# A two-layer decoder trunk with 32 experts: fewer slot groups, an earlier place for the norms' vectors, early fetches of the next layer's weights

## The chip, the cores and the metric

The kernel runs on one core of one Trainium2 chip. The metric is the device time of the whole program in microseconds (us), here the median of several runs.

## The reference, cut to what matters

Two layers work on 256 tokens of 1024 channels. In each, a token-mixing sublayer (one wide projection, two attentions, two gates, two branch projections and an output projection) is followed by a layer norm; then comes the channel sublayer, on which this change works:

```python
g_val, g_idx = lax.top_k(g_prob, 1)                 # one of 4 groups
e_val, e_idx = lax.top_k(e_prob, 2)                 # two of its 8 experts
for g in range(4):
    hg = silu(x @ w_g[g]) * (x @ w_u[g])            # 8 experts, 1024 -> 256
    y = y + (hg * comb[:, g]) @ w_d[g]              # 256 -> 1024
ple = sigmoid(x @ w_ple_gate) * (p @ w_ple)
x = layer_norm(alpha * x + y + ple, ln2_g, ln2_b)
```

So each layer has 32 experts, and each of the 256 tokens goes to two of them. All 32 experts' weights are read in each layer, 3 MB each.

## The kernel before, in words

**Places.** Nearly all of the on-chip memory is an arena of 47 places (`Arena`, L59; `Held`, L132), each as large as one weight tile of 512 KB. A tile that is to be loaded (`load=True`) takes the place that was given back longest ago, in the order of the program; any other takes one of the youngest free places, the fifth from the end. A transfer into a place can start only when the last reader of the former tenant is done. All weight transfers are issued on one queue, SP's, in the order of the program, so a transfer that waits for its place holds up all behind it.

**Slots and groups.** Tokens are gathered into 128 slots at a time, one group of experts. An expert has 64 or 32 slots, so a group is a pair (2 x 64) or a quad (4 x 32). The first `NFIX` experts (6) are taken by number, so that their weights can be fetched before the routing is known. The other experts are ranked by their number of tokens; those up to `NBIG` (12) get 64 slots, the others 32 (L878 to L889). That makes six pairs and five quads, eleven groups. `order` sets their order: P0 P1 P2 Q P3 Q P4 Q P5 Q Q. If an expert has more tokens than slots, `leftover` (L1183) runs loops over all experts; with these inputs it has nothing to do. Counted with the reference's own routing, the experts after the first four, ordered by tokens, have 45, 39, 28, 25, then at most 23 in the first layer and 39, 39, 33, 32, then at most 28 in the second; the first six have at most 45.

**A pass.** The loop at L1204 makes one pass for each group `gi`. In a pass TensorE (PE) does the gate and up products of the next group (`front(gi+1)`, L1126, which frees 4 tiles of each expert as it goes), the down products of this group (`back(gi)`, L1141, 2 tiles of each expert), the gather of the group after the next (`gather`, L899, into a place of its own), and the sum into the output (`combine`, L1068). A pair has 12 tiles, a quad 24, and PE's work on either is the same. The loads of ranked experts (`fetch`, L1030) are issued as `front` and `back` come to them in the program. In some passes (`early`, `e1`, `lastat`) units of the per-layer embedding are done as well (`Embed`, L732): two or three tiles for each quarter of the channels, a unit for each quarter and each half of the tokens. `e1` is pass 2; before, `early` is passes 4, 5, 6. In pass `ifat` (3) every engine branches on whether `leftover` has work.

**Around it.** Before the passes the fixed experts' tiles are fetched (L1111), then `nemb` further embeddings (L1116). In the pass before the last, `wide` (L379) takes two places for the last norm's gain and bias, loads 4 KB for each into one partition, and GpSimd (POOL) spreads them. `back(last)` (L1145) fetches the last group's down tiles. In the first layer it then fetches the first four tiles of the next layer's projection (`ahead`, L1147); after the norm's first steps ACT and POOL split these into the two parts that PE multiplies (L1271). `wide` also serves the first norm (L712), beside the router's weights `wr36` (L713).

Of the kernel before, what the change touches and what calls it, by code (L numbers as in the profile page):

```python
# [21 lines left out]
D = 1024  # L22
S = 256
DEPTH = 2
P = 128
KT = D // P
# [15 lines left out]
FAR = 1000.0  # L42


NFIX = 6
NBIG = 12


SEC = ["iq", "sq", "sk", "sv", "dq", "dk", "dv", "ga0", "ga1", "gb0", "gb1"]
# [30 lines left out]

@with_exitstack
def tile_hybrid_trunk(ctx: ExitStack, tc: tile.TileContext, x_in, xT_in, pT_in, pos_in, ws, wik, wrt, lnv,
                      brt, lamv, sublnv, out, places=47, t2b=4, young=4, gsb=1, hTb=1, silb=2, nring=5, early=(4, 5, 6), nahead=4, apart=8, npre=36, wA=1, wB=1, wC=1, wD=1, wE=3, inorder=2, e0=2, e1=2,  nearly_=0, peng_=1, ifat=3, im=0, df=0, dh=15, nol=0, diag=1, rpool='0000', lastemb=1, lastat=6, pre_if=(4,5), npair=6, fh=False, fg=0, order=(0,1,2,6,3,7,4,8,5,9,10), engs=None, nemb=1, nwarm=9, nfine=2, nah=4, o1=False, o2=False, o3=True, o4=True, order2=True, pa=2, pb=7, f1=True):
    nc = tc.nc
    V, A, G = nc.vector, nc.scalar, nc.gpsimd

    class Tensor:

        last = None
# [17 lines left out]
    def in_turn():  # L107

        return tc.issue_after(PE.last.ins)
# [14 lines left out]
    def bank():  # L124
        return ps.tile([P, 512], F32, tag="mm", bufs=4, name=nm("mm"))
# [6 lines left out]
    class Held:  # L132
# [11 lines left out]
        def free(self):  # L144
            arena.give(self.b)
# [16 lines left out]
    def load(l, i, shape):  # L162
        r = Held(shape, load=True)
        nc.sync.dma_start(r.t, ws[l, i])
        return r
# [41 lines left out]
    def split(hi, lo, src, eng=V):  # L207
        copied[0] = A.activation(hi, src, AF.Copy)  # L208
        copied[1] = eng.tensor_tensor(lo, src, hi, op=OP.subtract)  # L209
# [12 lines left out]
    ahead, ready = [], []  # L222
    nearly, peng = nearly_, peng_
# [30 lines left out]
    def constants():  # L254
# [14 lines left out]
        G.iota(kbon, pattern=[[-1, NE]], base=NE - 1, channel_multiplier=0, allow_small_or_imprecise_dtypes=True)  # L269
        V.tensor_scalar(kbon[:, :NFIX], kbon[:, :NFIX], 1.0e6, None, op0=OP.add)  # L270
        G.iota(kid[:, 0:1], pattern=[[0, 1]], base=0, channel_multiplier=1, allow_small_or_imprecise_dtypes=True)
        V.tensor_scalar(kid[:, 1:2], kid[:, 0:1], float(NFIX), 1.0e6, op0=OP.is_lt, op1=OP.mult)
        V.tensor_tensor(kid[:, 1:2], kid[:, 1:2], kid[:, 0:1], op=OP.subtract)
# [52 lines left out]
    def parts(w, ring=None, eng=V, old=False):  # L326

        if ring:
            ring.append(ring.pop(0))
        r = Held([2, 512], F32R, load=old, place=ring[-1] if ring else None)  # L330
        split(r.v[:, 0, :], r.v[:, 1, :], w, eng)
        return r
# [45 lines left out]

    def wide(i, l):  # L379

        r = Held([D])
        nc.sync.dma_start(r.v[0:1], lnv[l, i:i + 1])
        G.partition_broadcast(r.v, r.v[0:1])  # L383
        return r
# [68 lines left out]
    for l in range(DEPTH):  # L453
# [3 lines left out]
        ahead, ready = [], []  # L457
# [240 lines left out]
        for h in range(2):  # L698
# [10 lines left out]
            if h == 0:  # L709
                free(*gates[:2])  # L710
        free(yaT, ybT)
        lng, lnb = wide(0, l), wide(1, l)  # L712
        wr36 = Held([KT, 36])  # L713
        nc.sync.dma_start(wr36.v, wrt[l])
        o = [None, None]
        for h in range(2):
# [151 lines left out]
        def places_of(b, mask, cols):  # L868

            n = cols.stop - cols.start  # L870
            PE.matmul(b[:, 0:n], trib, mask[:, 0, :], start=True, stop=True)
            PE.matmul(b[:, n:2 * n], onesb, mask[:, 0, :], start=True, stop=False)
            PE.matmul(b[:, n:2 * n], trib, mask[:, 1, :], start=False, stop=True)
            V.scalar_tensor_tensor(posm[:, :, cols], mask, -FAR, b[:, :2 * n].rearrange("p (t e) -> p t e", t=TT),
                                   op0=OP.mult, op1=OP.add)


        groups = [[(r, 2, 64)] for r in range(0, 2 * npair, 2)]  # L878
        small = NBIG
        for r in range(2 * npair, NBIG):  # L880
            n = min(2, NE - small)
# [42 lines left out]
        def marks_of(gi):  # L924

            gs = wt([P, TT, P], F32, "gs", gsb)
            c = 0
            for r, n, w in groups[gi]:
                marked[0] = V.tensor_tensor(gs[:, :, c:c + n * w].rearrange("p t (e s) -> p t e s", e=n),
                                            iom[:, None, None, :w].to_broadcast([P, TT, n, w]),  # L930
                                            posm[:, :, r:r + n, None].to_broadcast([P, TT, n, w]), op=OP.is_equal)
                c += n * w
            return gs
# [17 lines left out]
        places = bank()  # L951
# [5 lines left out]
        with in_turn():  # L957
            places_of(places, mkf[:, :, :NFIX], slice(0, NFIX))
        gs = marks_of(0)
        with tc.issue_after(marked[0].ins):  # L960
# [24 lines left out]
            V.tensor_scalar(perm, iom[:NE, :NE], FAR, kcol[:, 2:3], op0=OP.add, op1=OP.is_equal)  # L985
            V.tensor_copy(cw[:, :, :NFIX], cbf[:, :, :NFIX])
        with in_turn():
# [8 lines left out]
        cmi = ids[:, NE:]  # L996
        V.tensor_scalar(ids[:, :NFIX], iom[0:1, :NFIX], FAR, None, op0=OP.add)
        V.tensor_copy(ids[:, NFIX:NE], b[0:1, 2 * NE + NFIX:3 * NE])
        over = cut(NE, rows=1)
        for c, n in (slice(0, NBIG), 64.0), (slice(NBIG, NE), 32.0):  # L1000
            V.tensor_scalar(over[:, c], b[0:1, 3 * NE + c.start:3 * NE + c.stop], n, None, op0=OP.subtract)
# [40 lines left out]
        def weights_of(gi, js):  # L1042
            for j in js:
                for r, _ in experts(gi):
                    if (r, j) not in fetched:
                        fetch(r, j)
            return [[fetched.pop((r, j)) for r, _ in experts(gi)] for j in js]
# [15 lines left out]
        def halves_of(yp):  # L1063
            y = t2([P, 512], F32R), t2([P, 512], F32R)
            split(*y, yp)
            return y
# [48 lines left out]
                        fetch(r, j)  # L1115
        for q in range(1, 1 + nemb):  # L1116
            emb[q] = Embed(q)

        def strips(gi):


            for i, (_, sl) in enumerate(experts(gi)):
                for c in range(sl.start, sl.stop, 32):
                    yield i, slice(c, c + 32)
# [16 lines left out]
        def back(gi, hT):  # L1141

            ysplit.clear()
            ysplits.clear()
            wr = weights_of(gi, range(4, 6))  # L1145
            if gi == last and l < DEPTH - 1:
                ahead.extend(load(l + 1, i, [2, 512]) for i in range(len(ahead), KT // 2))  # L1147
                ready.extend(parts(r.v[:, k, :], eng=G) for r in ahead[:nearly] for k in range(2))
            ys = []
            for h in range(2):  # L1150
                yp = bank()
                for f in range(2):
                    for i, sl in strips(gi):
                        PE.matmul(yp[sl, :], hT[:, f, sl], wr[f][i].v[:, h, :], start=f == 0, stop=f == 1)
                ys.append(halves_of(yp))
                ysplits.append(copied[0])
                ysplit.append(copied[1])
            free(*wr[0], *wr[1])
            return ys

        last = len(groups) - 1
# [21 lines left out]
        def leftover(most):  # L1183
            def onward(cols, n):
                V.tensor_scalar(posm[:, :, cols], posm[:, :, cols], float(n), None, op0=OP.add)

            with tc.If(most > 0, preferred_fallthrough_block=False):
                onward(slice(0, NBIG), -64)
                onward(slice(NBIG, NE), -32)
                with tc.For_i(0, 2, 1):  # L1190
                    with tc.For_i(0, NE, 1) as r:
                        rest(r)
                    onward(slice(0, NE), -P)
                onward(slice(0, NBIG), 64 + 2 * P)
                onward(slice(NBIG, NE), 32 + 2 * P)
# [8 lines left out]
        for gi in range(len(groups)):  # L1204
# [31 lines left out]
            if gi == last - 1:  # L1236
                lng, lnb = wide(2, l), wide(3, l)
                xn = [Held([D]) for _ in range(TT)]
                if l < DEPTH - 1:
                    xT = Split(KT)  # L1240
# [102 lines left out]
```

## Time and profile before

| | |
|---|---|
| time, median of 3 runs | 939.35 us (938.26 to 940.98) |
| the profiled execution, its own time | 940.85 us |
| its span, first to last instruction | 939.2 us |
| PE busy | 906.3 us (96%) |
| VectorE (DVE), ScalarE (ACT), POOL busy | 425.7, 347.9, 33.8 us |
| read from HBM | 278.70 MB, 298 GB/s over the span |
| mean granted TensorE clock | 0.994 |

How to read it: busy time of PE counts a matmul from its start to a modelled end, so a PE that works through small pieces as they arrive still looks busy. The mean rate of the transfers covers stages of very different load: the attention needs few weights, the experts need most of them. In the timelines a row is a run of like instructions: its start, its length, engine, line, operation, output and inputs, count, and in brackets the idle time before it with what ended that.

### The profile page before, as it was taken

The page shows a single profiled execution, that of the slowest core. Times are in us where ns is not written, and L with a number is a line of the kernel's source. Part 1 is how long each engine was busy: PE and PEld are TensorE (multiplying, and loading weights), DVE is VectorE, ACT ScalarE, POOL GpSimd, SP SyncE. Part 2 cuts the span into 40 slices and gives each one's busy share as a digit, 9 for nine tenths or more (in the row PEclk, how much of TensorE's full clock was granted, in tenths as well). Part 3 has the DMA queues.
Part 4 walks back from the last instruction along what each step waited for, and adds up shares of the span by engine and source line. Part 5 has one row for each costly group of instructions (what it writes and reads, how often), then busy time and mean ns, then how long its engine had stood idle before and what let it go on. Part 6 is the DMA issues. An engine that isn't in the chain of part 4 may idle for free. (4 is left out here: it accounts for less than half of the span.)

```text
span 939.2 us, 15942 instructions
## 1 busy us (share of the span) xinstructions
PE 906.3 (96%) x5761; PEld 604.4 (64%) x5761; DVE 425.7 (45%) x1068; ACT 347.9 (37%) x704; POOL 33.8 (4%) x37
## 2 busy tenths in 40 slices
PE   8999999999999999999899999999989999999994
PEld 5877777876556466554388777788855465666441
DVE  6797466775221111122468954668731212112124
ACT  6567676532211111111346666775221111111110
POOL 0000000000000000000410000001000000000010
PEclk9999999999999999999999999999999999999998
DMA  8995343777899999996999233357778999999943
GB/s 280 414 405 202 115 144 127 248 235 286 304 380 385 412 418 416 416 415 273 387 418 364 90 125 123 113 186 252 251 278 322 360 417 414 418 419 416 418 177 139
DMA packets 79013, 280.86 MB, mean 299 GB/s; under 512 B 9160, under 2 KB 9928, under 8 KB 78928
## 3 DMA queue, kind: packets, MB, share of 16 engines
q1 hardware_dynamic: 78784, 279.78, 77.9%
q8 instruction: 47, 0.77, 0.3%
q14 instruction: 38, 0.31, 0.1%
q10 hardware_dynamic: 144, 0.00, 0.0%
HBM read 278.70 MB, written 1.05 MB: 298 GB/s over the span
## 5 line engine op out<-in xcount | busy, mean ns | idle before, releaser
L92 PE MATMUL acc<-a,a 128*128 128x512 f32 x1440 | 352.3, 398 | 2.7 <-ACT a L208 2.0
L92 PEld LDWEIGHTS acc<-a,a 128*128 128x128 f32 x1440 | 265.7, 188 | 65.5 <-ACT a L208 3.3
L92 PE MATMUL mm<-a,a 128*32 128x512 f32 (+5 forms) x1776 | 237.6, 526 | 0.0
L208 ACT ACTIVATE a<-a 128x512 fp32r<-128x512 f32 (+1 forms) x247 | 150.7, 631 | 100.2 <-PE acc L92 69.2
L209 DVE TENSOR_TENSOR a<-a,a 128x512 fp32r<-128x512 f32 (+1 forms) x239 | 160.1, 690 | 51.2 <-ACT a L208 50.5
L92 PEld LDWEIGHTS mm<-a,a 128*32 128x32 f32 (+3 forms) x1776 | 110.7, 130 | 99.2 <-issue 86.8
L92 PE MATMUL mm<-a,hT 128*32 128x512 f32 x704 | 96.4, 603 | 8.8 <-DMA a<-ws 4.9
L92 PEld LDWEIGHTS mm<-gs,a 128*128 128x128 f32 x704 | 80.4, 192 | 17.2 <-PE mm L92 11.7
L92 PE MATMUL mm<-gs,a 128*128 128x128 f32 x704 | 84.7, 278 | 0.0
L1050 ACT ACTIVATE sil<-mm 128x256 f32<-128x256 f32 x22 | 8.4, 383 | 171.5 <-PE mm L92 156.2
L92 PEld LDWEIGHTS mm<-a,hT 128*32 128x32 f32 x704 | 25.3, 111 | 71.4 <-issue 55.9
L1051 DVE SCALAR_TENSOR_TENSOR sil<-sil,wsl,mm 128x256 f32<-128x256 f32 x22 | 10.6, 481 | 133.6 <-ACT sil L1050 133.4
L209 DVE TENSOR_TENSOR t<-mm,t 128x512 fp32r<-128x512 f32 x44 | 30.4, 692 | 68.6 <-ACT t L208 68.6
L208 ACT ACTIVATE t<-mm 128x512 fp32r<-128x512 f32 x44 | 26.3, 597 | 78.6 <-PE mm L92 78.6
L919 DVE CAST sT<-mm 128x256 fp32r<-128x256 f32 x22 | 9.3, 425 | 97.4 <-PE mm L92 97.4
L92 PE MATMUL acc<-t,sT 128*128 128x512 f32 x176 | 48.4, 410 | 0.0
L906 ACT ACTIVATE a<-mm 128x512 f32<-128x512 f32 x40 | 23.9, 597 | 50.1 <-PE mm L92 47.6
L92 PEld LDWEIGHTS acc<-t,sT 128*128 128x128 f32 x176 | 31.1, 189 | 9.0 <-issue 2.5
L763 DVE TENSOR_TENSOR sil<-sil,mm 128x256 f32<-128x256 f32 x16 | 6.7, 416 | 54.4 <-ACT sil L762 54.4
L548 ACT ACTIVATE t<-mm,mx 128x128 f32<-128x128 f32 (+1 forms) x64 | 26.0, 421 | 10.7 <-DVE mx L545 10.7
L762 ACT ACTIVATE sil<-mm 128x256 f32<-128x256 f32 x16 | 6.1, 383 | 63.7 <-PE mm L92 63.7
L383 POOL PARTITION_BROADCAST a<-a x8 | 10.6, 1356 | 511.0 <-DMA a<-lnv 279.6
(197 smaller groups left out, 644.6 us busy)
## 6 DMA issues: line engine op xcount, KB each, us to landing
a<-ws SPq DMA_DIRECT2D x523, 512.0 KB, 9.4
a<-x_in SPq DMA_DIRECT2D x2, 512.0 KB
out<-a SPq DMA_DIRECT2D x4, 256.0 KB, 2.7
a<-xT_in SPq DMA_DIRECT2D x3, 256.0 KB
a<-wik SPq DMA_DIRECT2D x2, 288.0 KB, 8.2
a<-ws SPq DMA_DIRECT2D x2, 256.0 KB, 4.3
pT<-pT_in SPq DMA_DIRECT2D x2, 256.0 KB
a<-wrt SPq DMA_DIRECT2D x2, 144.0 KB, 2.7
```

The costliest lines, as they stand in the source:

```text
L92: self.last = nc.tensor.matmul(*a, **k)
L208: copied[0] = A.activation(hi, src, AF.Copy)
L209: copied[1] = eng.tensor_tensor(lo, src, hi, op=OP.subtract)
L383: G.partition_broadcast(r.v, r.v[0:1])
L548: A.activation(e[:, i * nk:(i + 1) * nk], b[:, i * nk:(i + 1) * nk], AF.Exp, bias=mx[:, i:i + 1], accum_out=sums[i])
L762: A.activation(g, b[:, :256], AF.Sigmoid)
L763: V.tensor_tensor(g, g, b[:, 256:], op=OP.mult)
L906: A.activation(xg, b.rearrange("p (k s) -> p k s", k=4), AF.Copy)
L919: V.tensor_copy(sT, b[:, :2 * P].rearrange("p (t q) -> p t q", t=TT))
L1050: A.activation(sil, gu[:, :FE], AF.Sigmoid)
L1051: V.scalar_tensor_tensor(sil, sil, wsl, gu[:, :FE], op0=OP.mult, op1=OP.mult)
```

## The change

It alters the sizes and the order of the groups (four fixed experts, eight with 64 slots: four pairs and six quads, in the order P0 P1 P2 Q P3 Q Q Q Q Q), moves the embedding units one pass forward, fetches three further embeddings instead of one before the first pass, fetches the next layer's first four tiles there too, and lets `wide` and `wr36` take the longest free place.

```diff
-NFIX = 6
-NBIG = 12
+NFIX = 4
+NBIG = 8
...
-def tile_hybrid_trunk(..., early=(4, 5, 6), lastat=6, npair=6, order=(0,1,2,6,3,7,4,8,5,9,10), nemb=1, ...):
+def tile_hybrid_trunk(..., early=(3, 4, 5), lastat=5, npair=4, order=(0,1,2,4,3,5,6,7,8,9), nemb=3, ...):
...
     def wide(i, l):
-        r = Held([D])
+        r = Held([D], load=True)
         nc.sync.dma_start(r.v[0:1], lnv[l, i:i + 1])
         G.partition_broadcast(r.v, r.v[0:1])
...
-        wr36 = Held([KT, 36])
+        wr36 = Held([KT, 36], load=True)
...
         for q in range(1, 1 + nemb):
             emb[q] = Embed(q)
+        if l < DEPTH - 1:
+            ahead.extend(load(l + 1, i, [2, 512]) for i in range(KT // 2))
...
             wr = weights_of(gi, range(4, 6))
-            if gi == last and l < DEPTH - 1:
-                ahead.extend(load(l + 1, i, [2, 512]) for i in range(len(ahead), KT // 2))
-                ready.extend(parts(r.v[:, k, :], eng=G) for r in ahead[:nearly] for k in range(2))
             ys = []
```

(`nearly` is 0, so the last of the removed lines did nothing.)

## Rows read from the trace of the kernel before

**Rows 1.** The page: PE's busy time; the weight tiles' issues, median us to landing.
```profile
PE 906.3 (96%) x5761; PEld 604.4 (64%) x5761; DVE 425.7 (45%) x1068; ACT 347.9 (37%) x704; POOL 33.8 (4%) x37
...
a<-ws SPq DMA_DIRECT2D x523, 512.0 KB, 9.4
```
**Rows 2.** Timeline of PE: where fronts begin, and one back (408.23).
```profile
401.34 7.07 PE L92 MATMUL mm<-a,a 128*32 128x512 f32 x64
408.23 3.62 PE L92 MATMUL mm<-a,hT 128*32 128x512 f32 x32
...
418.19 2.35 PE L92 MATMUL mm<-a,a 128*32 128x512 f32 x20
...
765.81 1.90 PE L92 MATMUL mm<-a,a 128*32 128x512 f32 x10
...
811.95 1.90 PE L92 MATMUL mm<-a,a 128*32 128x512 f32 x10
...
839.17 1.90 PE L92 MATMUL mm<-a,a 128*32 128x512 f32 x10
```
**Rows 3.** Timeline of PE: the last group's down products and what follows, both layers.
```profile
459.37 0.73 PE L92 MATMUL acc<-t,sT 128*128 128x512 f32 x2
...
466.39 0.66 PE L95 MATMUL mm<-identr,a 128*128 128x128 f32 x4 [1.28 <-DVE a L414]
...
913.47 1.05 PE L92 MATMUL mm<-a,hT 128*32 128x512 f32 x2
...
918.01 1.04 PE L92 MATMUL mm<-a,hT 128*32 128x512 f32 x2 [1.61 <-DMA a<-ws]
...
922.97 2.76 PE L92 MATMUL mm<-a,hT 128*32 128x512 f32 x18 [0.16 <-DMA a<-ws]
925.66 2.22 PE L92 MATMUL acc<-t,sT 128*128 128x512 f32 x8
```
**Rows 4.** Timeline of SP's queue: start, length, line, tile and count of the issues.
```profile
217.08 0.33 SPq L164 DMA_DIRECT2D a<-ws  x1
228.87 91.40 SPq L1040 DMA_DIRECT2D a<-ws  x68
...
444.74 0.58 SPq L382 DMA_DIRECT2D a<-lnv  x2
445.54 3.11 SPq L1040 DMA_DIRECT2D a<-ws  x6
448.69 2.38 SPq L164 DMA_DIRECT2D a<-ws  x4
...
691.48 90.79 SPq L1040 DMA_DIRECT2D a<-ws  x68
...
815.05 78.07 SPq L1040 DMA_DIRECT2D a<-ws  x62
911.21 0.59 SPq L382 DMA_DIRECT2D a<-lnv  x2
912.02 3.12 SPq L1040 DMA_DIRECT2D a<-ws  x6
```
**Rows 5.** Stretches: length, busy time of each engine, PE clock, DMA share, GB/s.
```profile
228.90:288.90 60.00, 58.26 (x513) 30.32 (x505) 12.38 (x35) 10.91 (x20) 0.00 (x0) 1.00 0.89 327
288.90:436.90 148.00, 145.91 (x1084) 88.40 (x1084) 28.22 (x75) 25.96 (x54) 0.00 (x0) 0.99 1.03 415
...
691.50:751.50 60.00, 58.26 (x513) 30.32 (x505) 12.37 (x35) 10.91 (x20) 0.00 (x0) 1.00 0.88 328
751.50:899.50 148.00, 146.13 (x1075) 90.03 (x1072) 27.89 (x71) 26.43 (x56) 0.00 (x0) 1.00 1.02 416
```
**Rows 6.** Short stretches, with the same columns, and a PE row behind a wait.
```profile
312.00:316.00 4.00, 2.27 (x12) 0.69 (x16) 1.32 (x3) 0.17 (x1) 0.00 (x0) 0.72 1.03 410
...
916.00:920.00 4.00, 2.16 (x6) 0.27 (x4) 0.00 (x0) 0.00 (x0) 0.00 (x0) 1.00 0.96 339
...
313.73 5.31 PE L92 MATMUL mm<-a,hT 128*32 128x512 f32 x32 [2.09 <-DVEq L1187]
```

More of the change, by code (lines that the diff above doesn't have):

```diff
@@ L82, in tile_hybrid_trunk @@
 def tile_hybrid_trunk(ctx: ExitStack, tc: tile.TileContext, x_in, xT_in, pT_in, pos_in, ws, wik, wrt, lnv,
-                      brt, lamv, sublnv, out, places=47, t2b=4, young=4, gsb=1, hTb=1, silb=2, nring=5, early=(4, 5, 6), nahead=4, apart=8, npre=36, wA=1, wB=1, wC=1, wD=1, wE=3, inorder=2, e0=2, e1=2,  nearly_=0, peng_=1, ifat=3, im=0, df=0, dh=15, nol=0, diag=1, rpool='0000', lastemb=1, lastat=6, pre_if=(4,5), npair=6, fh=False, fg=0, order=(0,1,2,6,3,7,4,8,5,9,10), engs=None, nemb=1, nwarm=9, nfine=2, nah=4, o1=False, o2=False, o3=True, o4=True, order2=True, pa=2, pb=7, f1=True):
+                      brt, lamv, sublnv, out, places=47, t2b=4, young=4, gsb=1, hTb=1, silb=2, nring=5, early=(3, 4, 5), nahead=4, apart=8, npre=36, wA=1, wB=1, wC=1, wD=1, wE=3, inorder=2, e0=2, e1=2,  nearly_=0, peng_=1, ifat=3, im=0, df=0, dh=15, nol=0, diag=1, rpool='0000', lastemb=1, lastat=5, pre_if=(4,5), npair=4, fh=False, fg=0, order=(0,1,2,4,3,5,6,7,8,9), engs=None, nemb=3, nwarm=9, nfine=2, nah=4, o1=False, o2=False, o3=True, o4=True, order2=True, pa=2, pb=7, f1=True):
     nc = tc.nc
```

## The prediction, made before the changed kernel was run

> **What bounds the kernel now.** I read the page first: PE is busy for 96% of the span [rows 1], so the first guess is that PE's work is the time. Then I went through PE's timeline pass by pass. A pass without embedding takes 16.85 us (418.19 less 401.34), one with two embedding units 27.2 (839.17 less 811.95) [rows 2], and between them PE hardly waits. There are two exceptions. In the branch of pass 3 PE stands for 2.09 us [rows 6]. And the last `back`, which begins at 913.47 in the second layer and needs 3.62 us of matmuls [rows 2, 3], is not done before 925.66, because it waits for its tiles one at a time [rows 3]. SP's queue tells why: the 62 issues that start at 815.05 are over at 893.1, nothing is issued until 911.21, then come the two loads of the norm's vectors, and only then the last six weight tiles [rows 4]. `wide` had taken young places, which the second last `back` was still reading. The queue stood still for 18 us while places were free. The first layer does the same at 444.74.
>
> The queue itself comes next. In each layer the ranked loads begin when the ranks are known, which I call T0: 228.87 and 691.48 [rows 4]. In the 148 us that follow the first 60 it moved 415 and 416 GB/s [rows 5], which is 117 tiles of 0.524 MB, a pitch of 1.262 us a tile. In the first 60 us it moved 327 and 328 GB/s, 37.4 tiles, which would have taken 47.2 us at the pitch: 12.8 us were lost to the start and to places not yet free [rows 5]. So from T0 + 60 on the queue is full, and PE's lead over it is small. That is the state the change meets.
>
> **The change part by part.**
> *One group fewer.* It takes a pass of 16.85 us from PE in each layer. The experts and their bytes stay.
>
> *Four fixed experts instead of six.* Twelve tiles move behind T0: the queue now has 28 x 6 = 168 to bring there, 212.0 us at the pitch. Before it had 156 and five of embeddings. These five (`nemb`) and, in the first layer, the four of the next layer move ahead of T0, where the queue is idle anyway from 217.4 to 228.87 [rows 4]; twelve fixed tiles leave it, so T0 stays. They hold places, though. At the first pass the tenants were 36 fixed tiles, 5 of embeddings and 4 of activations: 2 of 47 free. Now they are 24 + 10 + 4, and 4 more in the first layer: 5 free there, 9 in the second.
>
> *What is lost at the start.* With 3 places more at T0 the queue gets three tiles further before it waits for PE, 3.8 us: 9.0 us lost in the first layer. With 7 more it is 8.8: 4.0 lost in the second. A second wait is new. Front(4) begins 74.3 us behind T0 (765.81 [rows 2]); pass 3 now holds the branch and two embedding units, 29.3 us, so front(5) begins at T0 + 103.6 and frees its first tiles 1.8 us later. The places given until then allow 5 + 48 (fronts) + 20 (backs) + 5 (embeddings) - 1 (the gathered slots) = 77 loads in the first layer and 81 in the second, and at its pitch the queue lands the 77th at 9.0 + 97.2 = 106. It runs nearly dry: two to four us. I take four, since the step from landing to matmul isn't in the sum otherwise. Bounds for all of this: 4.0 us in either layer without any further wait, or 12.8 + 4 in both.
>
> *The norms' vectors.* Their loads now find a free place and cost SP two short issues. What they held up by 18 us follows at once. What is late next is the queue's own pitch.
>
> *The last `back`.* After its last tile 2.7 us of matmuls remain (925.66 less 922.97 [rows 3]). So it ends at 228.87 + 212.0 + 9.0 + 4 + 2.7 = 456.6 in the first layer, where it was 459.37 [rows 3], and at 691.48 + 212.0 + 4.0 + 4 + 2.7 = 914.2 in the second, where it was 925.66. That is 2.8 and 11.5, together 14.3 us. PE alone would be through earlier by 22 and 13 us: 913.47 with 3.62 of matmuls and about 1 of the sum in between is 918 without the wait, 7.7 earlier than now; less 16.85 that is 901.2, and 434.8 in the first layer. So the queue bounds the last passes: a quad brings 24 tiles, 30.3 us, to 16.85 us of PE.
>
> *Next layer's first tiles.* Their fetch leaves the place at 448.69 [rows 4]. Behind the last `back` PE waits for DVE's norm (1.28 us at 466.39 [rows 3]), not for these tiles, so I cost their earlier arrival at nothing; without that cover it would be worth about a microsecond. *The first norm's vectors and router weights* lie before T0, where PE has no wait for a transfer: nothing. *Two more value loads a layer, other masks and limits, units a pass earlier*: nothing, SP needs about 0.5 us for an issue (3.11 for six [rows 4]) of the 1.262, and the units are as many as before. `leftover` stays empty, by the token counts.
>
> **The sum**: 940.85 us for the profiled execution less 14.3 is 926.5; the median of the runs lies 1.5 lower, so 925.0.
>
> A rule speaks against all this. The Trainium skill, "DMA: Bandwidth & Descriptors", section "Where 436 GB/s comes from", says that transfers from HBM are bound at about 358 GB/s for each core. By that 168 tiles would take 246 us, an estimate, the kernel would be at about 993, and no pass should have been taken off PE. The rows of the same queue with the same tiles show 415 and 416 [rows 5]; the measurement decides, and I give it no chance.
>
> **The rivals.**
> *Places run out* (0.10). The embeddings and the next layer's tiles hold 11 places that experts could use, and the extra free places help nothing: 12.8 + 4 us lost in both layers. Then the ends are 460.4 and 923.0, in all 1.7 us better: 937.6. For it: the queue does lose 12.8 us today [rows 5]. Against it: the first wait is counted in places, and there are more of them.
>
> *PE's clock* (0.07), the slower one. In the last passes PE starves, and the granted clock falls to the lower of its two levels, 1.2 of 2.4 GHz. A pass then takes up to 33.7 us, more than the 30.3 of its tiles, so PE is the bound again: 3.4 us in each of up to five starved passes, and 2.7 more behind each last tile, 22 in all, 947. It decides where the waits of a pass come in one piece, as in the branch of pass 3, and not one for each tile. For it: behind the 2.09 us wait the clock was 0.72 and 32 matmuls took 5.31 instead of 3.62 us [rows 2, 6]. Against it: from 916 to 920 PE was busy for 2.16 of 4 us at a clock of 1.00 [rows 6], since it had a piece to do for each tile that came. The Trainium skill, "TensorE: Matmul & The Clock Gate", Part 1 on the HAM clock gate, says that throttled is the default and activity releases it, which the 0.72 bears out and the 1.00 at half activity does not decide.
>
> *PE stays the bound* (0.02). The queue keeps up, and the kernel gains the 16.85 us and the 7.7 of the wait in each layer: 890. It would need 1.15 us a tile; no stretch shows it.
>
> *The change doesn't do what it says* (0.01): an expert overflows its slots and `leftover` runs, far slower. The counts exclude it for these inputs.
>
> **The numbers.** The forecast has 0.80. A measurement of this kernel can tell about 0.3%, 2.8 us, from no change. Faster: forecast and PE-bound, 0.82. Same: places run out, 0.10. Slower: clock and overflow, 0.08. The range: with 4.0 us lost in each layer and no second wait the gain would be 27.3, 912; I stop at 914. Above it takes in the rival of the places: 938.
>
> **What would show it.** PE's timeline should have ten fronts a layer; SP's queue no gap before the vectors, and 168 weight issues from T0 almost without one, at 415 GB/s until the end; the last passes should show PE waiting for tiles; the last `back` should end near 456 in the first layer and, counted from T0, 223 us behind it in the second. Wrong would be: gaps in the queue behind T0 + 60, a clock below 1 in the last passes, or a T0 that moved.

## The result, and the profile after

The changed kernel takes 929.11 us (median of 4 runs, 927.96 to 930.78) against 940.16 us for the kernel before on the same chip (4 runs): a ratio of 0.9883, with a 95% interval from 0.9856 to 0.9911. That is 11 us faster, where 14.3 were forecast. The profiled execution took 929.02 us and its span is 927.1 us, 12.1 shorter than before.

SP's queue first, in the timeline of the changed kernel: start, length, line, tile and count of the issues. These rows answer to [rows 4].

```profile
229.16 205.53 SPq L1040 DMA_DIRECT2D a<-ws  x160
435.57 1.53 SPq L382 DMA_DIRECT2D a<-lnv  x2
438.45 7.52 SPq L1040 DMA_DIRECT2D a<-ws  x8
446.07 0.37 SPq L466 DMA_DIRECT2D a<-wik  x1
...
689.57 201.51 SPq L1040 DMA_DIRECT2D a<-ws  x160
891.98 1.51 SPq L382 DMA_DIRECT2D a<-lnv  x2
894.52 7.78 SPq L1040 DMA_DIRECT2D a<-ws  x8
```

The queue no longer stands still for the vectors: 891.08 to 891.98 is all that lies between the weights and them. The 168 loads are there, T0 is where it was in the first layer (229.16, 228.87 before), and the next layer's first load is issued right behind the last expert's.

What the queue moved, by stretches of the changed kernel from T0 (length, busy times, PE clock, DMA share, GB/s in the last column), and one stretch of the last passes:

```profile
229.20:289.20 60.00, 58.26 (x513) 30.33 (x505) 12.38 (x35) 10.92 (x20) 0.00 (x0) 1.00 0.95 355
289.20:445.90 156.70, 150.96 (x1014) 83.10 (x1011) 26.07 (x71) 23.72 (x50) 2.48 (x2) 1.00 1.02 411
689.60:749.60 60.00, 58.26 (x513) 30.32 (x505) 12.39 (x35) 10.92 (x20) 0.00 (x0) 1.00 0.99 393
749.60:902.20 152.60, 148.60 (x1036) 86.39 (x1033) 26.68 (x72) 24.57 (x52) 2.38 (x2) 1.00 1.01 405
...
424.00:456.00 32.00, 28.74 (x132) 6.48 (x125) 2.56 (x6) 2.42 (x6) 2.48 (x2) 1.00 1.03 417
```

The first 60 us behind T0 now bring 355 and 393 GB/s, where they brought 327 and 328 [rows 5]. In tiles that is 40.6 and 45.0 of the 47.5 that the pitch of 1.262 us allows: 8.7 and 3.2 us are lost. In the last passes the queue runs at 417 GB/s without a hole, and PE does only 132 matmuls in 32 us; a pass without embedding does 144 in 16.85 us.

PE's timeline of the changed kernel in these passes (in brackets the idle time before a row and what ended it):

```profile
406.92 1.89 PE L92 MATMUL mm<-a,hT 128*32 128x512 f32 x6
409.03 1.04 PE L92 MATMUL mm<-a,hT 128*32 128x512 f32 x2 [0.22 <-DMA a<-ws]
410.29 1.04 PE L92 MATMUL mm<-a,hT 128*32 128x512 f32 x2 [0.22 <-DMA a<-ws]
...
454.35 2.76 PE L92 MATMUL mm<-a,hT 128*32 128x512 f32 x18 [0.18 <-DMA a<-ws]
457.05 0.73 PE L92 MATMUL acc<-t,sT 128*128 128x512 f32 x2
...
910.87 2.76 PE L92 MATMUL mm<-a,hT 128*32 128x512 f32 x18 [0.17 <-DMA a<-ws]
913.56 2.22 PE L92 MATMUL acc<-t,sT 128*128 128x512 f32 x8
```

From about 407 on in the first layer PE catches up with the queue in every pass. Then it uses each tile the moment it lands (two matmuls of 1.04 us, 0.2 us of waiting, one piece in 1.26 us, the queue's pitch) until the pass has other work for it, as from 416.8 to 427.9. The page of the changed kernel counts such a PE as busy, so its share is 96% as before [rows 1], though another resource sets the time:

```profile
PE 890.8 (96%) x5473; PEld 588.1 (63%) x5473; DVE 421.2 (45%) x1056; ACT 341.9 (37%) x692; POOL 33.4 (4%) x37
```

The 288 matmuls fewer than before [rows 1] are one pass of 144 in each layer, so the kernel does ten passes, and `leftover` has run none of its loops. The last `back` ends at 457.05 (459.37 before [rows 3]) and, in the second layer, 224.0 us behind T0 (234.2 before).

### The profile page after: what moved, and what is told of

The parts are those of the page before. It is cut to its first block, busy times and chain, and to the rows that moved or that the text cites. A ratio compares the mean times of both kernels' runs of the same rounds, so it can differ in the third digit from the quotient of the medians.

```text
span 927.1 us, 15397 instructions
## 1 busy us (share of the span) xinstructions
PE 890.8 (96%) x5473; PEld 588.1 (63%) x5473; DVE 421.2 (45%) x1056; ACT 341.9 (37%) x692; POOL 33.4 (4%) x37
## 5 line engine op out<-in xcount | busy, mean ns | idle before, releaser
L92 PE MATMUL mm<-a,a 128*32 128x512 f32 (+5 forms) x1648 | 229.2, 521 | 1.1 <-DMA a<-ws 1.1
L92 PEld LDWEIGHTS mm<-a,a 128*32 128x32 f32 (+3 forms) x1648 | 107.4, 132 | 96.9 <-issue 78.2
L92 PE MATMUL mm<-a,hT 128*32 128x512 f32 x640 | 102.5, 594 | 10.1 <-DMA a<-ws 5.2
L92 PEld LDWEIGHTS mm<-gs,a 128*128 128x128 f32 x640 | 73.1, 192 | 15.5 <-PE mm L92 10.9
L92 PE MATMUL mm<-gs,a 128*128 128x128 f32 x640 | 77.0, 278 | 0.0
L209 DVE TENSOR_TENSOR t<-mm,t 128x512 fp32r<-128x512 f32 x40 | 27.7, 692 | 78.3 <-ACT t L208 78.3
L208 ACT ACTIVATE t<-mm 128x512 fp32r<-128x512 f32 x40 | 23.9, 597 | 87.8 <-PE mm L92 87.8
L92 PE MATMUL acc<-t,sT 128*128 128x512 f32 x160 | 43.9, 410 | 0.0
L906 ACT ACTIVATE a<-mm 128x512 f32<-128x512 f32 x36 | 21.5, 597 | 45.2 <-PE mm L92 43.9
L92 PEld LDWEIGHTS acc<-t,sT 128*128 128x128 f32 x160 | 28.3, 189 | 7.4 <-DVE t L209 0.9
```

What stands on the lines that cost most here:

```text
L92: self.last = nc.tensor.matmul(*a, **k)
L906: A.activation(xg, b.rearrange("p (k s) -> p k s", k=4), AF.Copy)
```

## The experiments

Times of different experiments come from different runs, so they are compared by their ratio to the kernel before, and finer differences by the traces, counted from each layer's own T0. The stage ahead of the first T0, which most edits leave alone, put T0 between 229 and 232 in these traces; what moves it was not looked into.

**The vectors alone.** The kernel before, with eleven groups and six fixed experts, and only this edit:

```diff
-        r = Held([D])
+        r = Held([D], load=True)
...
-        wr36 = Held([KT, 36])
+        wr36 = Held([KT, 36], load=True)
```

> The kernel before, with nothing changed but the places of the norms' vectors and the router weights. Theory (the changed kernel gains because the queue no longer stands still, and is then bound by the queue, so that the pass taken from PE is worth little): the last back ends where PE's own work ends it, 7.7 us earlier in each layer (about 451.6 and 918.0 less 7.7), 924.8 in all against 940.2, so faster than the changed kernel's 929.1. Rival (the pass of 16.85 us taken from PE makes the gain): at most 3 us faster than before, 937 or more.

Measured: 926.31 us, a ratio of 0.9841 (0.9823 to 0.9859). In PE's timeline of this kernel, at the end of either layer:

```profile
448.56 3.64 PE L92 MATMUL mm<-a,hT 128*32 128x512 f32 x32
452.13 0.73 PE L92 MATMUL acc<-t,sT 128*128 128x512 f32 x2
...
907.73 3.64 PE L92 MATMUL mm<-a,hT 128*32 128x512 f32 x32
911.30 2.25 PE L92 MATMUL acc<-t,sT 128*128 128x512 f32 x8
```

The last `back` does its 32 matmuls in one piece, 3.64 us, without a wait. It ends 222.7 us behind T0 in the first layer, where before it ended 230.5 behind, and 226.5 in the second, where it was 234.2: 7.8 and 7.7 us. The edit also moves the first norm's vectors and the router weights, but the stretch that holds them, from the first layer's last `back` to the second T0, takes 232.7 us instead of 232.1, and the first T0 is no earlier (229.45, 228.87 before): the gain is not there. These two arguments alone give as much as the whole change or more; the intervals of the two ratios just touch (0.9859 and 0.9856), and by the traces the span is 2.2 us shorter.

**The change without the vectors.** The changed kernel with these two edits undone.

> The changed kernel, with the vectors and the router weights back in young places. Theory: the vectors' loads wait for the second last back, which ends at about 447 in the first layer and 903 in the second, and the six to eight tiles behind them follow then: the last back ends some 4 to 6.5 us later in each layer, 937 to 942. Rival (the pass taken from PE makes the gain): 929 to 932.

Measured: 938.06 us, a ratio of 0.9963 (0.9944 to 0.9982). SP's queue in the first layer of this kernel:

```profile
419.75 20.91 SPq L1040 DMA_DIRECT2D a<-ws  x17
449.44 0.58 SPq L382 DMA_DIRECT2D a<-lnv  x2
450.24 4.18 SPq L1040 DMA_DIRECT2D a<-ws  x6
```

The hole is back, 440.7 to 449.4, and in the second layer 899.7 to 908.9. The last `back` ends 233.8 and 227.9 us behind T0, 5.9 and 3.9 later than in the changed kernel. All the rest of the change, a pass of PE's work in each layer among it, is worth 3.5 us or so without the two edits, and nothing on top of them. So the gain is the vectors', and the rival that gave it to the group is out. What the pass alone would be worth stays open: no run takes it without the twelve tiles that move behind T0 with it.

**The next layer's tiles late.** In the changed kernel:

```diff
-        if l < DEPTH - 1:
-            ahead.extend(load(l + 1, i, [2, 512]) for i in range(KT // 2))
...
             wr = weights_of(gi, range(4, 6))
+            if gi == last and l < DEPTH - 1:
+                ahead.extend(load(l + 1, i, [2, 512]) for i in range(KT // 2))
```

> The changed kernel, with the next layer's first four tiles fetched at the last back again. Theory (places at T0 decide what the queue loses at the start): the first layer has 9 places instead of 5, loses 4 us instead of 9 and ends its last back at about 452 instead of 457; the four tiles land at about 452, ten us before PE uses them, so about 924. Rival (the early fetch pays, since the four tiles are late otherwise): no gain at the last back, or a gain that is given back as a wait ahead of the next layer's first projection, 929 or more.

Measured: 925.28 us, 0.9831 (0.9810 to 0.9851), clear of the changed kernel's interval. Two stretches of this kernel from T0, and PE at the end of its first layer:

```profile
229.70:289.70 60.00, 58.26 (x513) 30.32 (x505) 12.37 (x35) 10.92 (x20) 0.00 (x0) 1.00 0.99 391
289.70:441.80 152.10, 147.51 (x1014) 82.73 (x1011) 26.07 (x71) 23.85 (x50) 2.48 (x2) 1.00 1.02 409
```
```profile
452.81 0.73 PE L92 MATMUL acc<-t,sT 128*128 128x512 f32 x2
...
459.07 0.66 PE L95 MATMUL mm<-identr,a 128*128 128x128 f32 x4 [0.51 <-DVE a L414]
```

With four places more, the first 60 us bring 391 instead of 355 GB/s, 3.5 us lost instead of 8.7, and the last `back` ends 223.1 us behind T0 instead of 227.9. Behind it PE still waits for DVE's norm (0.51 us at 459.07) and not for the tiles. So the early fetch cost the first layer 4.8 us and gained nothing; this part of the change is a loss. In the second layer, whose loads the edit leaves as they were, the last `back` of this trace ends 225.1 us behind T0 instead of 224.0. Why was not looked into; differences of about 1 us between two traces are therefore not evidence by themselves.

**One embedding early, not three.** The changed kernel with `nemb=1`.

> The changed kernel with one embedding fetched before the first pass instead of three: five tiles more behind T0, five places more at T0. Theory (bytes behind T0 at 1.262 us a tile, and a start that can't lose less than 4 us): the first layer loses 5 us less at the start and brings 6.3 us more, 1.3 later; the second has nothing left to save and is 6.3 later; 936.7. Rival (places decide, not bytes): 4 to 5 us faster, 924 to 925.

Measured: 933.46 us, 0.9917 (0.9896 to 0.9939), an interval that overlaps the changed kernel's; by the traces the last `back` ends 0.3 us earlier behind T0 in the first layer and 2.8 later in the second. The stretches of this kernel from T0 of the second layer show why it is less than I expected:

```profile
688.90:748.90 60.00, 58.27 (x513) 30.32 (x505) 12.38 (x35) 10.92 (x20) 0.00 (x0) 1.00 1.00 401
748.90:904.00 155.10, 150.68 (x1037) 86.76 (x1034) 26.75 (x73) 24.71 (x52) 2.48 (x2) 1.00 1.03 417
```

At 401 GB/s the start loses 2.1 us, so 4 was no floor; and behind it the queue is full at 417 GB/s, where the changed kernel had 405. I read this as the places: those that the early embeddings held had made part of the second wait. No run separates it from the other order of the loads. Bytes behind T0 and places at T0 nearly cancel: neither theory had the size right.

**Fewer bytes, the same matmuls.** In the changed kernel:

```diff
-            loaded[0] = nc.sync.dma_start(fetched[r, j].t, src)
+            n = 512 if r >= NBIG else 1024
+            loaded[0] = nc.sync.dma_start(fetched[r, j].t[:, :n], src[:, :n])
...
-                    wr[kt // 2][i].v[:, kt % 2, :]
+                    wr[kt // 2][i].v[:, kt % 2 if groups[gi][0][2] == 64 else 0, :]
...
-                    wr[f][i].v[:, h, :]
+                    wr[f][i].v[:, h if groups[gi][0][2] == 64 else 0, :]
```

> The changed kernel; the experts with 32 slots load only the first half of each weight tile, and their matmuls read that half twice (the other half of these weights is left out of the computation). PE's work and the order of everything stay, the queue has 72 tiles' bytes less behind T0. Theory (the queue bounds the last passes): PE is the bound again, the last back ends some 206 to 210 us behind T0 in both layers instead of 228 and 224, in all 929.1 less 22 and less 14, about 893. Rival (PE is slow in the last passes for another reason, its clock or its own order): 915 or more.

Measured: 894.71 us, 0.9513 (0.9494 to 0.9532). The last `back` ends 205.1 and 211.2 us behind T0 (206 to 210 expected), where the changed kernel needs 227.9 and 224.0. In PE's timeline of this kernel a quad's pass, and the last `back`:

```profile
402.37 7.07 PE L92 MATMUL mm<-a,a 128*32 128x512 f32 x64
409.26 3.62 PE L92 MATMUL mm<-a,hT 128*32 128x512 f32 x32
...
419.22 7.07 PE L92 MATMUL mm<-a,a 128*32 128x512 f32 x64
...
433.06 3.63 PE L92 MATMUL mm<-a,hT 128*32 128x512 f32 x30
```

The passes are 16.85 us again (419.22 less 402.37), as before the change. With the same matmuls in the same order, fewer bytes alone give 35 us back: the queue bounds the last passes of the changed kernel, and the pass that was taken from PE can be cashed only if the tiles come sooner.

**The embedding units later.** What the queue still loses is the second wait. Three kernels: the units in passes 4, 5, 6 with the next layer's tiles late, the same with passes 5, 6, 7, and passes 4, 5, 6 alone on the changed kernel. The edit of the first, on top of the late tiles:

```diff
-early=(3, 4, 5), lastat=5
+early=(4, 5, 6), lastat=6
```

> The changed kernel with the next layer's tiles fetched late, as in the run before, and the embedding units in passes 4, 5, 6 instead of 3, 4, 5. Theory (the second wait of the queue, behind pass 3, comes from the units in that pass, while PE has time to spare in the last ones): the wait goes, 1.7 us in the first layer and 3.8 in the second by the rates, so 925.3 less 5.5, 919.8, and faster than both kernels. Rival (the wait is set by the branch of pass 3 or by the number of places, and later units delay the end): 925 or more.

> The same with the units in passes 5, 6, 7. Theory: the wait was gone already, the queue sets the end, and PE has slack until there: the same 919.8 within 2 us. Rival (units late in the layer are on PE's path): 923 or more.

> The changed kernel with the units in passes 4, 5, 6 alone, the next layer's tiles early as in the change. Theory: 929.1 less 5.5, 923.6, the first layer still losing some 9 us at its start. Rival: 929 or more.

Measured: 922.25 us (0.9811, 0.9794 to 0.9827), 920.87 us (0.9809, 0.9791 to 0.9827) and 926.07 us (0.9846, 0.9826 to 0.9865). SP's waits in the changed kernel between 775 and 795, then in the first of the three between 770 and 790 (total, times, longest):

```profile
SPq L1040 <- PE mm L92: 9.6, 5, 6.7
SPq L1040 <- DMA a<-ws: 4.6, 7, 0.8
```
```profile
SPq L1040 <- DMA a<-ws: 6.4, 10, 0.8
SPq L1040 <- PE mm L92: 6.2, 8, 3.0
```

The longest wait of the queue for a place that PE still reads falls from 6.7 to 3.0 us. The first layer's rate shows it too, in the second stretch of the first of these kernels:

```profile
289.50:442.00 152.50, 148.13 (x1032) 82.96 (x1024) 27.66 (x74) 24.49 (x51) 2.48 (x2) 1.00 1.03 416
```

With the tiles late, the last `back` ends 221.7 and 221.4 us behind T0 with the units in passes 4, 5, 6 (223.1 and 225.1 without the edit), and 221.5 and 221.3 with passes 5, 6, 7; 1.4 and 3.6 us for 1.7 and 3.8 expected. On the changed kernel itself it ends 226.1 and 221.4 behind T0 (227.9 and 224.0 without the edit).

The times gained less than that. 922.25 was to be 919.8, and 926.07 was to be 923.6; each of these two ratios has an interval that overlaps that of the same kernel without the edit (0.9810 to 0.9851 and 0.9856 to 0.9911). So what later units gain is seen in single traces, and the times don't show it. Both kernels with late tiles and later units are faster than the kernel before and the changed one, by some 18 us and some 7. Their intervals don't tell them apart, and they only just meet that of the vectors alone at its low end.

## Why the prediction was right

**The standstill of the queue**: right, and larger than the rest. The step that put 7.7 us on the wait of the last `back` [rows 3, 4] is what the vectors alone measured, 7.8 and 7.7. The prediction never set it apart, though: its sum goes by the queue's tiles.

**The queue as the new bound**: right. 168 tiles at the pitch of 1.262 us, PE waiting tile by tile, the page's PE busy share unchanged; with the bytes taken away it went to 894.7, where the rival in which PE stays the bound had put 890.

**What is lost at the start**: 9.0 and 4.0 us forecast, 8.7 and 3.2 measured; counting free places at T0 was enough.

**The second wait** was there, and its term was too small: four us were put in for each layer, with the step from the last landing to its matmul in them. By the rates behind the first 60 us (411 and 405 GB/s, 122.8 and 117.9 tiles) the wait cost 1.7 and 3.8. The 4.5 and 5.1 tiles that were left at the end of these stretches (445.90 and 902.20) need 5.7 and 6.5 us at the pitch, and PE began on the last of them 8.45 and 8.67 us later (454.35 and 910.87): another 2.7 and 2.2, which I put to the step. That is 4.4 and 6.0 instead of 4. In the second layer a part of it is the queue itself, whose rate falls to 303 GB/s from 908.2 to 909.2 and to 135 in the microsecond behind it, so how long the step itself is stays open. The prediction had also named a gap in the queue behind T0 + 60 as a sign that it was wrong, beside its own forecast of this wait. There was one, 6.7 us for one place, ended at T0 + 102 in the second layer, and it is this wait.

**The last `back`**: forecast at 456.6 in the first layer, 457.05 measured; in the second 222.7 us behind T0, 224.0 measured.

**The size**: 14.3 us forecast, 11 measured by the medians (8.4 to 13.5 by the interval) and 12.1 between the spans. Between the spans the 2.2 missing are 0.5 in the first layer, 0.4 between the last `back` and the next T0, and 1.3 in the second layer. The term at fault is the one above, 2.0 too small in the second layer, of which the start gives back 0.8. The other microsecond, between spans and medians, is within the scatter of the runs, and each of these shares is near the 1.1 us by which two traces differed without a known reason.

**Next layer's first tiles**: costed at nothing where they land, rightly, and their price was in the sum as places (5 free instead of 9). The late fetch shows that price, 4.8 us. What I did not draw from my own terms is the comparison with the vectors alone: 7.7 us in each layer make 924.0 on the scale of the forecast's 925.0, so the numbers already said that the rest of the change would bring nothing more.

**The rivals.** Places run out: no, the start improved. PE's clock: no, it stayed at 1.00 in the last passes of this trace, with their waits of 0.2 us tile by tile; but it did fall in the last `back` of another kernel, as the last section shows. The rule of the Trainium skill ("DMA: Bandwidth & Descriptors", "Where 436 GB/s comes from") that transfers from HBM are bound at about 358 GB/s for each core would have made the change slower: the trace disagrees, with 417 GB/s in the last passes. This kernel uses one core; what holds while others read, no run here shows. An overflow into `leftover`: no, by the count of matmuls.

## What to carry to other kernels

On a queue that issues in order, a transfer of 4 KB costs as much as its destination makes it wait, with everything behind it; choose its place by when the last reader is done and not by its size. Before taking work from the engine that looks busiest, price the next bound: here PE's lead over the transfers was some microseconds, and the change that took 17 us of its work from each layer brought 3.5 us without the vectors' places and nothing on top of them, since the queue's bytes set the end. Only with fewer bytes behind T0 did PE's work bound the passes again. A tile fetched early is paid for with its place for as long as it lies there, and it pays only where the queue would otherwise be idle and nothing else wants the place.

## What had not been expected of the hardware

Behind the same branch and the same wait of 2.09 us, the changed kernel's matmuls ran at full clock. A row of PE's timeline, then the stretch around it:

```profile
314.09 3.64 PE L92 MATMUL mm<-a,hT 128*32 128x512 f32 x32 [2.09 <-DVEq L1186]
```
```profile
312.00:316.00 4.00, 1.91 (x21) 0.81 (x24) 1.33 (x3) 0.38 (x1) 0.00 (x0) 1.00 1.04 425
```

Before, it was 5.31 us for the 32 matmuls at a clock of 0.72 [rows 6]. That is not the change's doing: of the ten traces of this document, four have the drop there in the first layer (the kernel before, the vectors alone, the change without the vectors, and the units in passes 5, 6, 7, with 5.31 to 5.34 us) and six have none (3.64 us), all behind a wait of 2.08 or 2.09 us. So the drop to the lower level was no fixed consequence of the wait. What decides it, these traces don't show. Where PE sets the pace behind the branch, as in the kernel before, these 1.7 us may be in the time; no run separates them.

The same holds for the last `back`, where the clock rival had its place. In the second layer of the change without the vectors:

```profile
917.09 6.52 PE L92 MATMUL mm<-a,hT 128*32 128x512 f32 x24 [1.42 <-DMA a<-ws]
```
```profile
916.00:920.00 4.00, 2.91 (x5) 0.50 (x6) 0.00 (x0) 0.00 (x0) 0.00 (x0) 0.68 0.91 365
```

Behind a wait of 1.42 us the clock went down to 0.68 in this stretch, and to 0.50, the lower level, from 918 to 920. The kernel before kept 1.00 behind 1.61 us [rows 3, 6]. So what the rival feared does happen when PE waits for tiles; in the changed kernel's trace it did not.
